# Triangular inverse in a gated DeltaNet kernel: masks applied to the products, refinement in 16-bit halves

## The chip, the cores and the metric

One core of a Trainium2 chip runs the kernel. The metric is device microseconds of one execution, the median of three runs. A second execution was taken with the hardware profiler; its rows are what the text below reads.

## The reference, cut to what matters

The program is one layer of a hybrid encoder on 2048 prompt frames and 64 frames of a running stream (2112 tokens, width 1024). One projection feeds a gated DeltaNet group (4 heads of 128) and a pooling group; one output projection, a residual and a SwiGLU block follow. The change lies in the DeltaNet group, in the inverse of a unit triangular matrix that each chunk of tokens needs:

```python
gamma = jnp.exp(jnp.where(lower_incl, G[..., :, None] - G[..., None, :], -jnp.inf))
kb = k * beta[..., None]
Lm = jnp.where(lower_strict, jnp.einsum('bhncd,bhnsd->bhncs', kb, k) * gamma, 0.0)
T = lax.linalg.triangular_solve(eye + Lm, jnp.broadcast_to(eye, Lm.shape),
                                left_side=True, lower=True)
u = jnp.einsum('bhncs,bhnsv->bhncv', T, v * beta[..., None])
w = jnp.einsum('bhncs,bhnsk->bhnck', T, kb * jnp.exp(G)[..., None])
```

The kernel works on chunks of 128 tokens, so it needs the inverse of I + Lm, 128 x 128, once for each head and chunk: 16 chunks x 4 heads for the prompt, and two for the 64 frames of the stream, where two heads share a 128 x 128 matrix.

## The kernel before

The tokens go through in four blocks of 512 (the first has the 64 stream frames beside it). For each block the kernel projects one output tile of the input projection after the other (matmuls into `pp`), convolves and gates the four heads, and runs the DeltaNet group. The output projection of the block before (`pz`) lies between. All of this is the first stage. The second is the SwiGLU block in three blocks of 704 tokens (`px`, `py`, `pz`, `d`, `dx` with operands `h`, `ws`, `wsd`), which is built as a fast matrix product with seven products for eight.

A dense product is made of three float32r matmuls on high and low parts, 512 columns each in most blocks. In this text "dense" means these.

A `Front` does the work of two chunks of one head that needs no state: it transposes k (`ptk`), spreads the decay over the partitions (`gb`), forms Gam = exp of the decay differences, the products of k with q and k (`gr`), and from them U, the strictly triangular matrix (tile `Gst` in the profile) for both chunks side by side (128 x 2 x 128). There are 32 such fronts for the prompt, and one for the stream (`_s`). Then it inverts:

- Level l = 0 to 6 (0 to 5 for the stream) joins diagonal blocks of size 2^l to blocks twice as large. POOL multiplies U with the level's 0/1 mask into 16-bit `Um`; PE multiplies it with the present inverse T (`py`); ACT casts this to 16 bits (`Yt`); PE multiplies with V, the transposed inverse, for T and for V (`pt`, four products of 128 columns); DVE subtracts the result from T and V (`TV`, 128 x 512).
- Refinement: the residual F = I - T - U T in float32 (`pf`, two products), then V + F V and V + F (V + F V) in float32 (`px`, two and two products). The result X is float32.

A `Head` then runs over the chunks in order, with the state S (`pk`, `po`).

The order of instructions is not that of the code. Every operation is recorded with a rank; the fronts' operations have the highest priority (`hot`). Class `Machine` then runs a list scheduler over all records of the program: it has a cost for each kind of operation (a 128-column float32 product, for one, is dearer than a 16-bit one), gives each engine the ready operation with the best rank, lets TensorE take dense products while others are not ready, and writes out one fixed order for each engine. All instructions come from that one place, so that the profile gives them all the same line, L278; tiles tell them apart. A tile's name in the profile is the name in the code without numbers and tags: `Yt_p` is `Yt` of a prompt front. Each of the three front slots (`NLEV`) has one PSUM bank for all of `py`, `pt`, `pf` and `px`.

Of the kernel before, what the change touches and what calls it, by code (L numbers as in the profile page):

```python
# [18 lines left out]
P = 128  # L19
# [5 lines left out]
C = 128  # L25
# [330 lines left out]
def hybrid_kernel(ctx, tc, a, o):  # L356
    nc = machine = Machine(tc.nc)
    act = nc.scalar.activation
    tt = nc.vector.tensor_tensor
    ts = nc.vector.tensor_scalar  # L360
    stt = nc.vector.scalar_tensor_tensor
# [76 lines left out]
    cp1, gp = pool("cp1", p1, True), pool("gp", p1, True)  # L438
# [396 lines left out]
    nc.vector.tensor_copy(selp, names["sel"].unsqueeze(2))  # L835
    lm_f = gp.tile([P, 2, 512], F32, tag="Yqk", name="lm_f", bufs=NY).rearrange("p i (l n) -> p (i l) n", n=P)
    nc.sync.dma_start(out=lm_f, in_=a["lmask"])
    lmask = cp1.tile([P, 7, P], F16, tag="lmask", name="lmask")
    nc.vector.tensor_copy(lmask, lm_f[:, :7])
    negm = cp1.tile([P, P], BF16, tag="negm", name="negm")  # L840
    nc.vector.tensor_copy(negm, lm_f[:, 7])

# [17 lines left out]
    def bc(t, nch, n):  # L860
        return t.unsqueeze(1).to_broadcast([t.shape[0], nch, n])
# [4 lines left out]
    class Front:  # L866
# [43 lines left out]
        def all(self):  # L910
            tag, chunk = self.tag, self.chunk
            two = lambda ps: ps[:, : 2 * C].rearrange("p (c n) -> p c n", n=C)
            gt = lambda shape, dt, t, bufs, n="": gp.tile(shape, dt, tag=t, name=f"{t.split('_')[0]}{n}_{tag}", bufs=bufs)
            slot = self.i % NLEV
            lev = lambda dt, t, n="", shape=[P, 2, C], bufs=1: gt(shape, dt, f"{t}_{slot}", bufs, n)
            yield self.before(NOUT, "used")

            kn = self.kn = gt([P, 3, 2], F32, "kn", NOUT + 1)
            ktl = self.ktl = gt([P, 2, P], F32, "ktl", NOUT)
            ptr = self.ps(f"ptk_{tag}")  # L920
            for c in range(2):
                transpose(ptr[:, c * P : (c + 1) * P], chunk(1, c), ident)
            for c in range(2):
                act(ktl[:, c, :], ptr[:, c * P : (c + 1) * P], AF.Square, accum_out=kn[:, 2, c : c + 1])
            for c in range(2):
                act(ktl[:, c, :], ptr[:, c * P : (c + 1) * P], AF.Copy, scale=self.e(2)[:, c : c + 1])
            act(kn[:, 2], kn[:, 2], AF.Ln, bias=epsc)
            act(kn[:, 0], kn[:, 2], AF.Exp, scale=0.5)
            act(kn[:, 1], kn[:, 2], AF.Exp, scale=-1.0)
            tt(kn[:, 1], kn[:, 1], self.e(1), ALU.mult)  # L930
            ts(kn[:, 2], kn[:, 1], -1.0, None, ALU.mult)
            yield self.before(NLEV, "levels")
            TV32 = lev(F32, "TV32", "", [P, 2, 2, C])
            gb = self.ps(f"gb_{tag}")
            self.rowmm(gb)
            EG = TV32[:, 0]
            act(EG, two(gb), AF.Exp)
            EL = self.EL = gt([P, NH if self.h is None else 2, 1], F32, "EL", NOUT)
            n = DEC if self.h is None else C
            nc.gpsimd.tensor_copy(EL, EG.rearrange("p c n -> p (c n)").rearrange("p (e n) -> p e n", n=n)[:, :, n - 1 : n])  # L940
            Qd = self.Qd = gt([P, 2, C], F32, "Qd", NOUT)
            tt(Qd, self.Yqk[:, 0, self.off : self.off + 2 * C].rearrange("p (c n) -> p c n", n=C), EG, ALU.mult)

            mm(gb[:, : 2 * C], idbf, bc(negm2 if self.h is None else negm, 2, C), start=False, stop=True,
               skip_group_check=True)
            Gam = self.QKG = gt([P, 2, C], F32, "Gam", NOUT)
            for c in range(2):
                act(Gam[:, c], gb[:, c * C : (c + 1) * C], AF.Exp, bias=self.fall()[:, c : c + 1])
            U = lev(F32, "Gst")
            nc.gpsimd.tensor_tensor(out=U, in0=Gam, in1=bc(ident, 2, C), op=ALU.subtract)  # L950
            yield LAT_G
            ps = self.ps(f"gr_{tag}")
            for c in range(2):
                ck = slice(self.off + c * C, self.off + (c + 1) * C)
                mm(ps[:, c * 2 * C : (c + 1) * 2 * C], chunk(1, c), self.Yqk[:, :, ck], start=True, stop=True)
            v = ps.rearrange("p (c t n) -> p c t n", t=2, n=C)
            for c in range(2):
                stt(U[:, c], v[:, c, 1, :], kn[:, 1, c : c + 1], U[:, c], ALU.mult, ALU.mult)
            tt(Gam, v[:, :, 0, :], Gam, ALU.mult)
            yield LAT_G  # L960

            TV = None
            nlev = n.bit_length() - 1
            for l in range(nlev):
                Um = lev(F16, "Um", l, bufs=2)
                nc.gpsimd.tensor_tensor(out=Um, in0=U, in1=bc(lmask[:, l], 2, C), op=ALU.mult)
                new = TV32 if l == nlev - 1 else lev(F16, f"TV{l % 2}", l, [P, 2, 2, C])
                py = self.ps(f"py{l}_{tag}")  # L970
                for c in range(2):
                    mm(py[:, c * C : (c + 1) * C], Um[:, c], id16 if l == 0 else TV[:, 0, c], start=True, stop=True)
                if l == 0:
                    idb = bc(id16, 2, C)
                    tt(new[:, 0], idb, two(py), ALU.subtract)
                    nc.gpsimd.tensor_tensor(out=new[:, 1], in0=idb, in1=Um, op=ALU.subtract)
                else:
                    Yt = lev(F16, "Yt", l)
                    nc.scalar.copy(Yt, two(py))
                    yield LAT_A  # L980
                    pt = self.ps(f"pt{l}_{tag}")
                    for c in range(2):
                        mm(pt[:, c * C : (c + 1) * C], TV[:, 1, c], Yt[:, c], start=True, stop=True)
                    for c in range(2):
                        mm(pt[:, (c + 2) * C : (c + 3) * C], Yt[:, c], TV[:, 1, c], start=True, stop=True)
                    tt(new, TV, pt.rearrange("p (t c n) -> p t c n", t=2, n=C), ALU.subtract)
                TV = new
                yield LAT_TV
            T, V = TV32[:, 0], TV32[:, 1]

            F = lev(F32, "TV0", "F")
            nc.gpsimd.tensor_tensor(out=F, in0=bc(ident, 2, C), in1=T, op=ALU.subtract)
            pf = self.ps(f"pf_{tag}")
            for c in range(2):
                mm(pf[:, c * C : (c + 1) * C], U[:, c], T[:, c], start=True, stop=True)
            tt(F, F, two(pf), ALU.subtract)
            yield LAT_F
            px = self.ps(f"px0_{tag}")
            for c in range(2):
                mm(px[:, c * C : (c + 1) * C], F[:, c], V[:, c], start=True, stop=True)  # L1000
            tt(T, V, two(px), ALU.add)
            yield LAT_D
            yield self.before(NX, "used")
            X = self.X = gt([P, 2, C], F32, "X", NX)
            px = self.ps(f"px1_{tag}")
            for c in range(2):
                mm(px[:, c * C : (c + 1) * C], F[:, c], T[:, c], start=True, stop=True)
            tt(X, V, two(px), ALU.add)
            self.levels = True

            ptr2 = self.ps(f"ptv_{tag}")
            vtk = self.vtk = gt([P, 2, P], F32, "vtk", NX)
            for c in range(2):
                transpose(ptr2[:, c * P : (c + 1) * P], chunk(2, c), ident)
            for c in range(2):
                act(vtk[:, c, :], ptr2[:, c * P : (c + 1) * P], AF.Copy, scale=kn[:, 0, c : c + 1])
            yield LAT_D
            self.done = True
# [401 lines left out]
    for k in (4, 5, 6, 7, 0, 1, 2, 3):  # L1420
        t = wpool.tile([P, 512], F32, tag="xc", name=f"od{k}", bufs=XBUFS["xc"])
# [271 lines left out]
def _layout(inp):  # L1693
# [51 lines left out]
    lm = np.zeros((P, 8, P), f32)  # L1745
    for l in range(7):
        s = 1 << l
        lm[:, l, :] = (i[:, None] // (2 * s) == i[None] // (2 * s)) & (i[:, None] // s < i[None] // s)
    lm[:, 7, :] = np.where(i[None] >= i[:, None], 0.0, -1e30)
    r["lmask"] = lm  # L1750
    z = np.zeros((P, 12), f32)
# [47 lines left out]
```

## Time and profile before

| | |
|---|---|
| median of three runs | 2381.3 us (2381.26 to 2382.45) |
| span of the profiled execution, first to last instruction | 2378.0 us |
| granted TensorE clock over the span | 0.998 |
| level and refinement work, first to last | 68 to 930 us |
| first product of the SwiGLU stage | 977.9 us |
| busy: TensorE, VectorE, ScalarE, GpSimd | 98%, 75%, 54%, 43% |

No total of the profiled execution other than its span is at hand; the difference of 3.3 us to the median is what the runs count before and after the first and last instruction. PE is TensorE, PEld its weight loads, DVE VectorE, ACT ScalarE, POOL GpSimd. A row of a group reads: operation, written tile, read tiles, shape and type, count, busy time in us, mean duration in ns, idle time of the engine just before these and what ended it. A row of the timeline has the start in us, the time that the merged instructions cover, and their count; a number in brackets is idle time before. A float32 product of 128 columns has two records, a 16-bit one has one. Matmuls overlap in the pipeline, so their cost is read from start to start.

### The profile page before, as it was taken

Reading aid. Unit: us, or ns where it says so; the run is one execution under the profiler, and the core shown is the slowest. Engines: PE = TensorE matmul, PEld = TensorE weight load, DVE = VectorE, ACT = ScalarE, POOL = GpSimd, SP = SyncE. Lnnn points to the kernel's source line nnn. Section 1 sums busy time; section 2 is a strip of 40 time slices with the busy share of each in tenths; the row PEclk is TensorE's granted clock in tenths of the full one; section 3 lists DMA queues with packets and bytes.
Section 4 is the critical chain, followed back from the end, with each engine's and each line's share of the span. In section 5 each row is a group of like instructions: output and inputs, shape, how many; then the busy total and the mean of one; then the engine's idle time right before and its main releaser. Section 6 shows DMA issues by size and latency. Waiting matters only on the chain. (4 is left out here: it accounts for less than half of the span.)

```text
span 2378.0 us, 41860 instructions
## 1 busy us (share of the span) xinstructions
PE 2331.7 (98%) x14679; PEld 2176.7 (92%) x14679; DVE 1775.5 (75%) x3096; ACT 1288.2 (54%) x2920; POOL 1011.0 (43%) x1160
## 2 busy tenths in 40 slices
PE   8999999999999999999999999999999999999998
PEld 8898898878787868999999999999999999999998
DVE  8998875775677786788676764878777778777666
ACT  6766745572647464574453555664444564545444
POOL 3756633553357552354232225554323563323122
PEclk9999999999999999999999999999999999999999
DMA  8744565545555565887654556766744586454653
GB/s 292 250 152 164 164 226 207 174 153 183 170 196 181 174 197 161 307 284 240 211 182 169 186 194 228 255 218 194 254 163 149 168 292 215 148 180 161 201 177 107
DMA packets 218883, 471.37 MB, mean 198 GB/s; under 512 B 27185, under 2 KB 85553, under 8 KB 218673
## 3 DMA queue, kind: packets, MB, share of 16 engines
q1 hardware_dynamic: 218672, 468.71, 58.9%
q8 instruction: 115, 1.88, 0.3%
q14 instruction: 96, 0.78, 0.1%
HBM read 354.81 MB, written 113.80 MB: 197 GB/s over the span
## 5 line engine op out<-in xcount | busy, mean ns | idle before, releaser
L278 PE MATMUL pp<-h,wsp 128*128 128x512 f32 (+1 forms) x2480 | 560.6, 366 | 10.3 <-DVE wsp L278 9.8
L278 PEld LDWEIGHTS pp<-h,wsp 128*128 128x128 f32 x2480 | 401.5, 190 | 57.0 <-ACT wsp L278 9.2
L278 POOL TENSOR_TENSOR Um_p<-Gst_p,lmask 128x256 f16<-128x256 f32 x224 | 181.3, 823 | 98.6 <-PE py_p L278 76.3
L278 ACT CAST ws<-wr 128x512 fp32r<-128x512 f32 x198 | 121.9, 618 | 175.5 <-PE dx L278 50.0
L278 DVE TENSOR_TENSOR ws<-wr,ws 128x512 fp32r<-128x512 f32 x198 | 168.1, 851 | 55.3 <-ACT ws L278 51.0
L278 PE MATMUL pz<-op,wsp 128*128 128x288 f32 (+1 forms) x768 | 170.0, 358 | 1.0 <-ACT op L278 0.5
L278 PE MATMUL d<-h,wsd 128*128 128x352 f32 x1056 | 170.0, 322 | 0.0
L278 PEld LDWEIGHTS d<-h,wsd 128*128 128x128 f32 x1056 | 168.7, 188 | 0.1
L278 DVE TENSOR_TENSOR TV_p<-TV_p,pt_p 128x512 f16<-128x512 f16 x192 | 129.3, 680 | 33.2 <-PE pt_p L278 31.4
L278 ACT ACTIVATE hr<-g 128x352 f32<-128x352 f32 x132 | 65.6, 497 | 158.9 <-DVE g L278 158.6
L278 POOL TENSOR_TENSOR wrS<-wr,wrS 128x512 f32<-128x512 f32 x44 | 64.9, 1476 | 196.5 <-DMA wrS<-in_wu_dram 65.8
L278 PE MATMUL px<-hA,ws 128*128 128x352 f32 x792 | 145.0, 322 | 0.6 <-DVE ws L278 0.6
L278 PE MATMUL px<-hBT,wsS 128*128 128x352 f32 x792 | 139.8, 324 | 5.5 <-ACT g L278 5.0
L278 PE MATMUL py<-hB,wsS 128*128 128x352 f32 x792 | 143.6, 322 | 0.0
L278 PE MATMUL pz<-hB,ws 128*128 128x352 f32 x792 | 142.0, 322 | 0.0
L278 PE MATMUL py<-hA,wsS 128*128 128x352 f32 x792 | 140.0, 322 | 0.0
L278 PE MATMUL px<-hBT,ws 128*128 128x352 f32 x792 | 138.4, 323 | 1.5 <-DVE u L278 1.4
L278 PE MATMUL px<-hA,wsS 128*128 128x352 f32 x792 | 137.9, 322 | 1.4 <-ACT g L278 1.3
L278 PEld LDWEIGHTS px<-hBT,wsS 128*128 128x128 f32 x792 | 128.0, 188 | 10.7 <-ACT g L278 10.7
L278 POOL TENSOR_TENSOR q<-hr,hr 128x352 f32<-128x352 f32 x40 | 44.0, 1099 | 216.2 <-DVE hr L278 214.7
L278 PEld LDWEIGHTS pz<-op,wsp 128*128 128x128 f32 x768 | 120.6, 190 | 12.3 <-DVE wsp L278 0.8
L278 PEld LDWEIGHTS px<-hBT,ws 128*128 128x128 f32 x792 | 128.4, 188 | 3.4 <-DVE u L278 3.2
(672 smaller groups left out, 5858.0 us busy)
## 6 DMA issues: line engine op xcount, KB each, us to landing
wsS<-gS SPq DMA_DIRECT2D x176, 512.0 KB, 4.5
wsp<-wnd SPq DMA_DIRECT2D x126, 512.0 KB, 3.3
gS<-wsS SPq DMA_DIRECT2D x88, 512.0 KB, 4.3
wr<-in_wg_dram SPq DMA_DIRECT2D x132, 256.0 KB, 3.0
wnd<-wsp SPq DMA_DIRECT2D x42, 512.0 KB, 5.0
xd<-x2d SPq DMA_DIRECT2D x96, 176.0 KB, 3.4
wr<-in_wu_dram SPq DMA_DIRECT2D x66, 256.0 KB, 3.4
wrd<-in_wd_dram SPq DMA_DIRECT2D x56, 256.0 KB, 3.0
```

What stands on the lines that cost most here:

```text
L278: getattr(getattr(self.nc, op.eng), name)(*args, **kw)
```

## The change

The diagonal is put into the matrix: U becomes 2048 (I + Lm)^T, with POOL's addition of a scaled identity (`idw`), and ACT casts it once to 16 bits (`Wh`); POOL forms the low half `Wl` = U - `Wh`. Every level multiplies the whole `Wh` with T, and DVE applies the level's mask when it takes the product out of PSUM. The masks are now I minus the 0/1 block mask, divided by 2048, so that the masked product is the factor with which T and V are multiplied; `pt` then gives the new T and V themselves, and ACT casts them out of PSUM (128 x 512). T and V stay in 16 bits at the last level too. An eighth mask, the transpose of level 0's, is made once by one product.

The refinement: `pf` = `Wh` T + `Wl` T in four 16-bit products; F = I - pf/2048 on DVE; F scaled by 256 is split into a high half (ACT) and a low half (DVE); `px` = F V in four 16-bit products; ACT casts it (`YtF`), and two further products with the high half accumulate F F V onto it; DVE adds V. The result X is float32 as before.

```diff
@@ setup
-    lmask = cp1.tile([P, 7, P], F16, tag="lmask", name="lmask")
-    nc.vector.tensor_copy(lmask, lm_f[:, :7])
+    lmask = cp1.tile([P, 8, P], F16, tag="lmask", name="lmask")
+    nc.vector.tensor_copy(lmask[:, :7], lm_f[:, :7])
...
+    idw = cp1.tile([P, P], F16, tag="idw", name="idw")
+    ts(idw, ident, WSCALE, None, ALU.mult)
+    pm = bank(0, "pm")
+    mm(pm[:, :P], lmask[:, 0], id16, start=True, stop=True)
+    nc.scalar.copy(lmask[:, 7], pm[:, :P])
@@ Front.all
-            tt(kn[:, 1], kn[:, 1], self.e(1), ALU.mult)
-            ts(kn[:, 2], kn[:, 1], -1.0, None, ALU.mult)
+            stt(kn[:, 1], kn[:, 1], WSCALE, self.e(1), ALU.mult, ALU.mult)
+            ts(kn[:, 2], kn[:, 1], -1.0 / WSCALE, None, ALU.mult)
...
+            nc.gpsimd.tensor_tensor(out=U, in0=U, in1=bc(idw, 2, C), op=ALU.add)
+            Wh = lev(F16, "Wh")
+            nc.scalar.copy(Wh, U)
...
             for l in range(nlev):
-                Um = lev(F16, "Um", l, bufs=2)
-                nc.gpsimd.tensor_tensor(out=Um, in0=U, in1=bc(lmask[:, l], 2, C), op=ALU.mult)
-                new = TV32 if l == nlev - 1 else lev(F16, f"TV{l % 2}", l, [P, 2, 2, C])
+                new = lev(F16, f"TV{l % 2}", l, [P, 2, 2, C])
                 py = self.ps(f"py{l}_{tag}")
                 for c in range(2):
-                    mm(py[:, c * C : (c + 1) * C], Um[:, c], id16 if l == 0 else TV[:, 0, c], start=True, stop=True)
+                    mm(py[:, c * C : (c + 1) * C], Wh[:, c], id16 if l == 0 else TV[:, 0, c], start=True, stop=True)
+                Z = new[:, 0] if l == 0 else lev(F16, "Yt", l)
+                tt(Z, two(py), bc(lmask[:, l], 2, C), ALU.mult)
                 if l == 0:
-                    idb = bc(id16, 2, C)
-                    tt(new[:, 0], idb, two(py), ALU.subtract)
-                    nc.gpsimd.tensor_tensor(out=new[:, 1], in0=idb, in1=Um, op=ALU.subtract)
+                    nc.gpsimd.tensor_tensor(out=new[:, 1], in0=Wh, in1=bc(lmask[:, 7], 2, C), op=ALU.mult)
                 else:
-                    Yt = lev(F16, "Yt", l)
-                    nc.scalar.copy(Yt, two(py))
...
-                    tt(new, TV, pt.rearrange("p (t c n) -> p t c n", t=2, n=C), ALU.subtract)
+                    nc.scalar.copy(new, pt.rearrange("p (t c n) -> p t c n", t=2, n=C))
+                if l == 1:
+                    Wl = lev(F16, "Wl")
+                    nc.gpsimd.tensor_tensor(out=Wl, in0=U, in1=Wh, op=ALU.subtract)
...
-            F = lev(F32, "TV0", "F")
-            nc.gpsimd.tensor_tensor(out=F, in0=bc(ident, 2, C), in1=T, op=ALU.subtract)
             pf = self.ps(f"pf_{tag}")
             for c in range(2):
-                mm(pf[:, c * C : (c + 1) * C], U[:, c], T[:, c], start=True, stop=True)
-            tt(F, F, two(pf), ALU.subtract)
+                for w in (Wh, Wl):
+                    mm(pf[:, c * C : (c + 1) * C], w[:, c], T[:, c], start=w is Wh, stop=w is Wl)
+            F = lev(F32, "TV32", "F")
+            stt(F, two(pf), -1.0 / WSCALE, bc(ident, 2, C), ALU.mult, ALU.add)
+            FF = lev(F16, f"TV{nlev % 2}", "F", [P, 2, 2, C])
+            act(FF[:, 0], F, AF.Copy, scale=FSCALE)
+            stt(FF[:, 1], F, FSCALE, FF[:, 0], ALU.mult, ALU.subtract)
...
-                mm(px[:, c * C : (c + 1) * C], F[:, c], V[:, c], start=True, stop=True)
-            tt(T, V, two(px), ALU.add)
...
-                mm(px[:, c * C : (c + 1) * C], F[:, c], T[:, c], start=True, stop=True)
-            tt(X, V, two(px), ALU.add)
+                for i in range(2):
+                    mm(px[:, c * C : (c + 1) * C], FF[:, i, c], V[:, c], start=c == i == 0, stop=i == 1,
+                       skip_group_check=c > 0)
+            FV = lev(F16, "Yt", "F")
+            act(FV, two(px), AF.Copy, scale=1.0 / FSCALE)
+            yield LAT_D
+            for c in range(2):
+                mm(px[:, c * C : (c + 1) * C], FF[:, 0, c], FV[:, c], start=False, stop=True, skip_group_check=True)
+            stt(X, two(px), 1.0 / FSCALE, V, ALU.mult, ALU.add)
@@ host tables
+WSCALE, FSCALE = 2048.0, 256.0
...
-        lm[:, l, :] = (i[:, None] // (2 * s) == i[None] // (2 * s)) & (i[:, None] // s < i[None] // s)
+        lm[:, l, :] = (i[:, None] == i[None]) * 1.0 - ((i[:, None] // (2 * s) == i[None] // (2 * s)) & (i[:, None] // s > i[None] // s))
+        lm[:, l, :] /= WSCALE
```

The scheduler's costs and rules stay as they are; since the operations differ, it writes another order. First TensorE's order where the residual of one front is formed (third block, second head, first two chunks), before. `TV_p_1_0` is that front's T and V, `pz` the dense product between:

```order
L278 MATMUL pz_4_0_1786<-op_1_1229,wsp_64_1701 128x512 x3
L278 MATMUL pk_p_0_1_1834<-Sp,Yqk_0_1518 128x128
L278 MATMUL pf_p_1_0_1837<-TV_p_1_0_1709,Gst_p_1_0_1714 128x128 x2
L278 LDWEIGHTS TV_p_1_1_1825
L278 MATMUL pt_p_1_1_1844<-Yt_p_1_1_1841,TV_p_1_1_1825 128x128
```

The same place after the change:

```order
L278 MATMUL pt_p_1_1_1770<-TV_p_1_1_1747,Yt_p_1_1_1768 128x128
L278 LDWEIGHTS Wh_p_1_0_1673
L278 MATMUL pf_p_1_0_1777<-TV_p_1_0_1763,Wh_p_1_0_1673 128x128
L278 LDWEIGHTS Wl_p_1_0_1704
L278 MATMUL pf_p_1_0_1777<-TV_p_1_0_1763,Wl_p_1_0_1704 128x128
```

Two float32 products with U became 16-bit ones with `Wh` and `Wl` (four in all, two for each chunk), right behind the 16-bit `pt` of the neighbouring front.

Second, ScalarE's order at the end of the same front, before:

```order
L278 CAST Yt_p_1_1_1827<-py_p_1_1_1826 128x256
L278 ACTIVATE vn_p_0_1_1820<-pk_p_0_1_1816,kn_p_0_1_1609 128x128
L278 CAST Yt_p_1_0_1823<-py_p_1_0_1822 128x256
L278 CAST Yt_p_1_1_1841<-py_p_1_1_1840 128x256
L278 ACTIVATE vn_p_0_1_1842<-pk_p_0_1_1834,kn_p_0_1_1609 128x128
```

and after:

```order
L278 CAST TV_p_1_0_1763<-pt_p_1_0_1769 128x512
L278 CAST TV_p_1_1_1766<-pt_p_1_1_1770 128x512
L278 ACTIVATE TV1F_p_1_0_1779<-TV32F_p_1_0_1778 128x256
L278 ACTIVATE vn_p_0_1_1783<-pk_p_0_1_1771,kn_p_0_1_1558 128x128
L278 ACTIVATE YtF_p_1_0_1787<-px_p_1_0_1786 128x256
```

ScalarE now takes `pt` (512 columns) instead of `py` (256 columns), and has two casts of the refinement beside the head's `vn`.

Third, GpSimd's order at the start of a front of the first block (fourth head, first two chunks), before:

```order
L278 TENSOR_TENSOR Gst_p_3_0_684<-Gam_p_3_0_683,consts 128x256
L278 TENSOR_TENSOR Um_p_3_0_714<-Gst_p_3_0_684,lmask 128x256
L278 TENSOR_TENSOR Um_p_3_0_729<-Gst_p_3_0_684,lmask 128x256
L278 TENSOR_TENSOR TV_p_3_0_715<-id_144,Um_p_3_0_714 128x256
L278 TENSOR_TENSOR Um_p_3_0_749<-Gst_p_3_0_684,lmask 128x256
L278 TENSOR_TENSOR Um_p_3_0_767<-Gst_p_3_0_684,lmask 128x256
```

and after:

```order
L278 TENSOR_TENSOR Gst_p_3_0_669<-Gam_p_3_0_668,consts 128x256
L278 TENSOR_TENSOR osq_p_1__603<-osq_p_1__603,Yvz_1_200 128x512
L278 TENSOR_TENSOR Gst_p_3_0_669<-Gst_p_3_0_669,idw 128x256
L278 TENSOR_TENSOR TV_p_3_0_704<-Wh_p_3_0_696,lmask 128x256
L278 TENSOR_TENSOR Wl_p_3_0_727<-Gst_p_3_0_669,Wh_p_3_0_696 128x256
```

One product with a mask for each level became three operations per front, all near its start.

More of the change, by code (lines that the diff above doesn't have):

```diff
@@ L929, in all @@
             act(kn[:, 1], kn[:, 2], AF.Exp, scale=-1.0)
-            tt(kn[:, 1], kn[:, 1], self.e(1), ALU.mult)
-            ts(kn[:, 2], kn[:, 1], -1.0, None, ALU.mult)
+            stt(kn[:, 1], kn[:, 1], WSCALE, self.e(1), ALU.mult, ALU.mult)
+            ts(kn[:, 2], kn[:, 1], -1.0 / WSCALE, None, ALU.mult)
             yield self.before(NLEV, "levels")
-            TV32 = lev(F32, "TV32", "", [P, 2, 2, C])
+            EG = lev(F32, "TV32", "")
             gb = self.ps(f"gb_{tag}")
             self.rowmm(gb)
-            EG = TV32[:, 0]
             act(EG, two(gb), AF.Exp)
@@ L958, in all @@
                 stt(U[:, c], v[:, c, 1, :], kn[:, 1, c : c + 1], U[:, c], ALU.mult, ALU.mult)
+            nc.gpsimd.tensor_tensor(out=U, in0=U, in1=bc(idw, 2, C), op=ALU.add)
+            Wh = lev(F16, "Wh")
+            nc.scalar.copy(Wh, U)
             tt(Gam, v[:, :, 0, :], Gam, ALU.mult)
             yield LAT_G
-            TV = None
             nlev = n.bit_length() - 1
             for l in range(nlev):
-                Um = lev(F16, "Um", l, bufs=2)
-                nc.gpsimd.tensor_tensor(out=Um, in0=U, in1=bc(lmask[:, l], 2, C), op=ALU.mult)
-                new = TV32 if l == nlev - 1 else lev(F16, f"TV{l % 2}", l, [P, 2, 2, C])
+                new = lev(F16, f"TV{l % 2}", l, [P, 2, 2, C])
                 py = self.ps(f"py{l}_{tag}")
                 for c in range(2):
-                    mm(py[:, c * C : (c + 1) * C], Um[:, c], id16 if l == 0 else TV[:, 0, c], start=True, stop=True)
+                    mm(py[:, c * C : (c + 1) * C], Wh[:, c], id16 if l == 0 else TV[:, 0, c], start=True, stop=True)
+                Z = new[:, 0] if l == 0 else lev(F16, "Yt", l)
+                tt(Z, two(py), bc(lmask[:, l], 2, C), ALU.mult)
                 if l == 0:
-                    idb = bc(id16, 2, C)
-                    tt(new[:, 0], idb, two(py), ALU.subtract)
-                    nc.gpsimd.tensor_tensor(out=new[:, 1], in0=idb, in1=Um, op=ALU.subtract)
-                else:
-                    Yt = lev(F16, "Yt", l)
-                    nc.scalar.copy(Yt, two(py))
+                    nc.gpsimd.tensor_tensor(out=new[:, 1], in0=Wh, in1=bc(lmask[:, 7], 2, C), op=ALU.mult)
+                else:
                     yield LAT_A
@@ L982, in all @@
                     for c in range(2):
-                        mm(pt[:, c * C : (c + 1) * C], TV[:, 1, c], Yt[:, c], start=True, stop=True)
+                        mm(pt[:, c * C : (c + 1) * C], TV[:, 1, c], Z[:, c], start=True, stop=True)
                     for c in range(2):
-                        mm(pt[:, (c + 2) * C : (c + 3) * C], Yt[:, c], TV[:, 1, c], start=True, stop=True)
-                    tt(new, TV, pt.rearrange("p (t c n) -> p t c n", t=2, n=C), ALU.subtract)
+                        mm(pt[:, (c + 2) * C : (c + 3) * C], Z[:, c], TV[:, 1, c], start=True, stop=True)
@@ L987, in all @@
+                    nc.scalar.copy(new, pt.rearrange("p (t c n) -> p t c n", t=2, n=C))
+                if l == 1:
+                    Wl = lev(F16, "Wl")
+                    nc.gpsimd.tensor_tensor(out=Wl, in0=U, in1=Wh, op=ALU.subtract)
                 TV = new
                 yield LAT_TV
-            T, V = TV32[:, 0], TV32[:, 1]
-            F = lev(F32, "TV0", "F")
-            nc.gpsimd.tensor_tensor(out=F, in0=bc(ident, 2, C), in1=T, op=ALU.subtract)
+            T, V = TV[:, 0], TV[:, 1]
@@ L993, in all @@
             pf = self.ps(f"pf_{tag}")
             for c in range(2):
-                mm(pf[:, c * C : (c + 1) * C], U[:, c], T[:, c], start=True, stop=True)
-            tt(F, F, two(pf), ALU.subtract)
-            yield LAT_F
-            px = self.ps(f"px0_{tag}")
-            for c in range(2):
-                mm(px[:, c * C : (c + 1) * C], F[:, c], V[:, c], start=True, stop=True)
-            tt(T, V, two(px), ALU.add)
-            yield LAT_D
+                for w in (Wh, Wl):
+                    mm(pf[:, c * C : (c + 1) * C], w[:, c], T[:, c], start=w is Wh, stop=w is Wl)
@@ L1003, in all @@
+            F = lev(F32, "TV32", "F")
[3 more added lines that the diff above has]
+            stt(FF[:, 1], F, FSCALE, FF[:, 0], ALU.mult, ALU.subtract)
+            yield LAT_F
             yield self.before(NX, "used")
             X = self.X = gt([P, 2, C], F32, "X", NX)
-            px = self.ps(f"px1_{tag}")
+            px = self.ps(f"px_{tag}")
```

## The prediction

> **What bounds the kernel now.** I read the page first, then busy time by stage, then TensorE's waits, then its instructions one by one.
>
> ```profile
> PE 2331.7 (98%) x14679; PEld 2176.7 (92%) x14679; DVE 1775.5 (75%) x3096; ACT 1288.2 (54%) x2920; POOL 1011.0 (43%) x1160
> ```
>
> TensorE (PE) is busy for 98% of the span; no other engine comes near over the whole. An average hides stages, so here is the same by stage: length, then busy time of PE, weight loads, DVE, ACT and POOL, then granted clock and DMA share.
>
> ```profile
> 70.00:200.00 130.00, 127.62 (x1037) 118.46 (x1036) 125.36 (x259) 94.34 (x255) 85.11 (x119) 1.00 0.59 199
> 200.00:300.00 100.00, 98.66 (x660) 82.45 (x658) 90.08 (x165) 64.56 (x153) 66.05 (x80) 1.00 0.51 169
> 300.00:800.00 500.00, 498.68 (x3150) 419.10 (x3148) 337.82 (x614) 269.31 (x695) 233.19 (x328) 1.00 0.54 183
> 800.00:900.00 100.00, 93.29 (x509) 73.77 (x508) 86.00 (x139) 58.91 (x146) 60.68 (x71) 0.97 0.67 204
> 900.00:978.00 78.00, 78.00 (x432) 66.07 (x431) 55.91 (x100) 39.11 (x84) 15.91 (x15) 1.00 0.66 207
> 978.00:2378.00 1400.00, 1376.30 (x8497) 1359.93 (x8495) 1023.08 (x1687) 713.13 (x1470) 522.42 (x496) 1.00 0.60 201
> ```
>
> Everything that the change touches ends by 978 us; from there the SwiGLU stage runs, whose rows on PE stand in the same order in both programs. Up to 978 PE is the bound too: the five rows hold 11.7 us without PE work (908 less 896.3). From 70 to 300 us DVE runs close behind, at 215 of 230 us. What PE waited for from 10 to 970 us (total, times, longest; the five largest):
>
> ```profile
> PE pt_p L278 <- ACT Yt_p L278: 3.7, 4, 2.0
> PE py_p L278 <- DVE TV_p L278: 2.2, 2, 1.9
> PE gb_p L278 <- ACT ktl_p L278: 1.9, 4, 0.6
> PE pf_p L278 <- DVE TV_p L278: 1.3, 2, 0.7
> PE pp L278 <- DVE wsp L278: 0.6, 1, 0.6
> ```
>
> 9.7 us, and little behind them. So hundreds of handovers between the level products and ACT or DVE cost PE some 7 us in all: the list scheduler puts dense matmuls (pp, pz) into the gaps. A microsecond of PE work taken out before 978 us is then a microsecond of time, and the sum below is one of PE work.
>
> **Removed and added on PE.** Now the price of one product. First how many float32 products the refinement has, then PE's starts around one front.
>
> ```profile
> L278 PE MATMUL px_p<-TV_p,TV0F_p 128*128 128x128 f32 x256 | 40.2, 278 | 0.0
> L278 PE MATMUL pf_p<-TV_p,Gst_p 128*128 128x128 f32 x128 | 21.1, 284 | 1.3 <-DVE TV_p L278 1.3
> ...
> 661.72 0.61 PE L278 MATMUL px_p<-TV_p,TV0F_p 128*128 128x128 f32 x4
> 662.16 0.28 PE L278 MATMUL pt_p<-Yt_p,TV_p 128*128 128x128 f16 x2
> 662.27 0.28 PE L278 MATMUL pt_p<-TV_p,Yt_p 128*128 128x128 f16 x2
> 662.38 0.66 PE L278 MATMUL px_p<-TV_p,TV0F_p 128*128 128x128 f32 x4
> ...
> 820.69 0.38 PE L278 MATMUL pk_p<-vn_p,ktl_p 128*128 128x128 f32 x2
> 820.91 0.39 PE L278 MATMUL po_p__2584<-Gam_p,vn_p 128*128 128x128 f32 x2
> 821.05 2.78 PE L278 MATMUL pp<-h,wsp 128*128 128x512 f32 x11
> 823.67 0.38 PE L278 MATMUL pk_p<-Sp,Yqk 128*128 128x128 f32 x2
> ...
> 849.14 0.29 PE L278 MATMUL py_p<-TV_p,Um_p 128*128 128x128 f16 x2
> 849.24 1.86 PE L278 MATMUL pp<-h,wsp 128*128 128x512 f32 x7
> 850.94 0.23 PE L278 MATMUL pt_p<-Yt_p,TV_p 128*128 128x128 f16 x1
> ```
>
> 384 records over 32 fronts are twelve for six products: a float32 product is two records. The busy times (278 ns) overlap, so I take start to start. From 661.72 to 662.16 two float32 products take 0.44 us; from 820.69 to 820.91 one takes 0.22. Two 16-bit products take 0.11 (662.16 to 662.27): 0.055 each, with new weights for each. The 33 fronts (32 and the sample's) lose 6 x 33 = 198 float32 products, 198 x 0.22 = 43.6 us, and gain 10 x 33 + 1 = 331 16-bit ones, 331 x 0.055 = 18.2. The level products keep their number and size. Net -25.4 us.
>
> Changing the kind of product costs too. Eleven dense matmuls take 2.62 us up to a float32 product and seven take 1.70 up to a 16-bit one, so one is 0.23 and entering either kind costs 0.09. Going back is cheaper: after a float32 product dense work starts 0.14 later instead of 0.22 (-0.08), after 16-bit ones 0.10 instead of 0.11 (-0.01). Counted in the two orders, PE leaves dense work for 16-bit products 273 times instead of 180 and for float32 ones 179 instead of 264 (+8 x 0.09 = +0.7), returns from 16-bit ones 302 times instead of 267 (-0.4) and from float32 ones 149 instead of 176 (27 x 0.08 = +2.2). Together +2.5.
>
> **Moved between the other engines.** The rows with the prices:
>
> ```profile
> L278 DVE TENSOR_TENSOR TV_p<-TV_p,pt_p 128x512 f16<-128x512 f16 x160 | 108.0, 680 | 27.6 <-PE pt_p L278 26.1 <-POOL Um_p L278 1.2
> L278 DVE TENSOR_TENSOR TV_p<-id,py_p 128x256 f16<-128x256 f16 x32 | 13.1, 410 | 0.5 <-PE py_p L278 0.5
> L278 DVE TENSOR_TENSOR TV_p<-TV_p,px_p 128x256 f32<-128x256 f32 x32 | 13.3, 416 | 8.0 <-PE px_p L278 7.4
> L278 DVE SCALAR_TENSOR_TENSOR h<-x,nw,h 128x288 fp32r<-128x288 f32 x16 | 7.1, 511 | 4.7 <-ACT h L278 4.7
> L278 ACT CAST Yt_p<-py_p 128x256 f16<-128x256 f32 x192 | 70.4, 373 | 110.4 <-PE py_p L278 110.0
> L278 ACT COPY ext<-pp 128x512 f32<-128x512 f32 x36 | 20.9, 579 | 19.0 <-PE pp L278 18.8
> L278 ACT CAST wsp<-wrp 128x256 fp32r<-128x256 f32 x4 | 1.4, 403 | 0.4 <-DMA wrp<-in_win_dram 0.4
> L278 ACT ACTIVATE E<-E,onec 128x512 f32<-128x512 f32 x64 | 46.8, 732 | 1.3
> L278 POOL TENSOR_TENSOR Um_p<-Gst_p,lmask 128x256 f16<-128x256 f32 x224 | 181.3, 823 | 98.6 <-PE py_p L278 76.3 <-DVE Gst_p L278 21.1 <-POOL Um_p L278 0.3
> ```
>
> - DVE, per front: six 128x512 updates (6 x 0.68) go and six masked products of half the width come (6 x 0.41). The three narrow adds of the refinement (0.416) become three scalar_tensor_tensor of 256 columns; no row has that shape, the 288-column one (0.511) is the ceiling, a 256-column add at 0.41 the floor, and I take 0.47. -1.5 us a front.
> - ACT: six casts (0.373) become six of twice the width out of PSUM (0.579), and three of 256 columns are new (0.37 to 0.403). +2.4 us a front, 80 in all, over a stage in which ACT works 526 of 908 us.
> - POOL: seven mask products and F go, the addition of idw and Wl come; the start of V stays. Six fewer at 0.823: -5 us a front.
> - A level's chain stays as long: cast 0.373 and update 0.68 before, mask 0.41 and cast 0.579 now. The front's start gets an ACT cast longer (U, idw on POOL, Wh on ACT, where U, Um stood), its end a cast and a DVE step longer between pf and px (+0.4 + 0.47). Both lie on the front's own chain, and dense matmuls cover that as they now cover each level's cast and update; without cover PE would pay up to 33 x 1.3 = 43 us. Behind a cast that waits for py or pt stand silu's E (up to 0.73) and the copies that free PSUM for pp.
> - The set-up's one product, its copy to the eighth mask and idw lie in the first 45 us beside dense work: 0, at most their own microsecond. No DMA is added or moved past another, and the mask table keeps its size.
>
> **The sum.** -25.4 + 2.5 = -22.9. Of the waits, 7.2 us belong to handovers that now change engines; I take 1 us off, since POOL's mask products drop out and DVE is relieved where it ran at 215 of 230 us. The span of 2378.0 becomes 2354.1; the median of the runs, 2381.3, lies 3.3 above that span, and I keep the difference: 2357.
>
> **A page against a row.** How fast 16-bit products with new weights each can follow one another decides most of the added term; this is the weight load's row (count, least, median and longest ns):
>
> ```profile
> L278 PEld LDWEIGHTS <-Yt_p x384: 95/98/147, 73.1 to 922.9; 128*128 128x128 f16 x192
> ```
>
> The loads are longer than the 0.055 between starts, yet the starts are 0.055 apart: they overlap. The Trainium skill ("TensorE: Matmul & The Clock Gate", Back-to-back issue gap) states about 81 ns a product for a stream of load and matmul pairs at 128 columns. By it the added term would be an estimated 331 x 0.081 = 26.8 and the time 2366; the trace's 0.055 disagrees.
>
> **Rivals.**
> 1. *The load sets the pace after all*, in these pairs of high and low halves: 331 x 0.098 = 32.4, net -11.2 + 2.5 - 1, 2372. Against it stands every pair of pt above. The Trainium skill's figure above leans this way. 0.04.
> 2. *ACT answers late* (the other side). Place: the cast of pt to the new T and V, 197 times, on which the next py waits; an E of 0.73 may stand ahead of it. From 70 to 200 us ACT goes from 94 of 130 us to about 109 of 125. Price: if PE stands for an E at a quarter of them, 50 x 0.73 = 36 us, and the time is 2393; it decides from 24 us, 0.12 a handover. A wait also costs afterwards:
>
> ```profile
> 803.61 0.39 PE L278 MATMUL po_p__2584<-Gam_p,vn_p 128*128 128x128 f32 x2
> 805.99 0.27 PE L278 MATMUL pt_p<-Yt_p,TV_p 128*128 128x128 f16 x2 [2.00 <-ACT Yt_p L278]
> ...
> 806.18 2.25 PE L278 MATMUL pp<-h,wsp 128*128 128x512 f32 x5
> 808.23 0.63 PE L278 MATMUL pk_p<-Sp,Yqk 128*128 128x128 f32 x2
> ```
>
>    After 2 us of idleness five dense matmuls took 2.05 us up to the next float32 product instead of 5 x 0.23 + 0.09 = 1.24. Against it: the same handover runs through ACT now, 192 times, and cost 3.7 us in four waits, while ACT idled 110 us for py. 0.20, in which 0.07 ends still faster, 0.06 within the bound, 0.07 slower.
> 3. *More comes than the products*: lighter DVE and POOL end nearly all waits in the stage, 10 us and a microsecond of slow clock: 2346. For it, 215 of 230 us on DVE; against it, ACT's load. 0.14.
> 4. *The saving lies off the path from 70 to 300 us*, since DVE is the bound there. Some nine fronts run in that stretch, 9 x 0.7 = 6 us lost: 2363. DVE loses 1.5 us where PE loses 0.7, so it should not; I count it inside the forecast's own range.
>
> **How the numbers follow.** 0.62 for the forecast, 2357, whose own range is 2351 to 2364 (rival 4 above; a float32 product at 0.225 and three more waits gone below). The range of 8 in 10 reaches from rival 3 to rival 1: 2345 to 2372. 0.2% is 4.8 us, about what a measurement of this kernel can tell from no change. Faster by more: 0.62 + 0.14 + 0.04 + 0.07 = 0.87; within: 0.06; slower: 0.07.
>
> **What would show it.** PE's records pf_p and px_p are f16, in pairs 0.11 apart; the SwiGLU stage starts near 954 us instead of 978 and lasts 1400 again; PE's waits before it stay near 12 us; ACT's busy time rises by some 80 us, DVE's falls by some 50 and POOL's by some 160. Wrong would be a row of PE waiting for ACT's TV_p or YtF_p with tens of microseconds, 16-bit pairs 0.16 apart or more, or a later stage that grows.

## The result, and the profile after

The changed kernel takes 2344.9 us (median of 4 runs, 2343.8 to 2345.7) against 2381.3 beside it: ratio 0.985 (0.984 to 0.986). That is 36.4 us less where 24 were forecast: on the lower edge of the range of 8 in 10 (2345 to 2372) and below the forecast's own range (2351 to 2364). Its profiled execution has a span of 2342.9 us, 35.1 less than before, and a granted clock of 0.999.

The page's first line (busy time and share of the span, engine by engine):

```profile
PE 2304.3 (98%) x14614; PEld 2139.1 (91%) x14614; DVE 1688.4 (72%) x3097; ACT 1357.9 (58%) x3020; POOL 840.9 (36%) x963
```

ACT gained 70 us of work; DVE lost 87 and POOL 170. By stage (length, then busy PE, weight loads, DVE, ACT, POOL, clock, DMA share, GB/s):

```profile
70.00:200.00 130.00, 128.50 (x1092) 118.94 (x1092) 120.72 (x278) 110.12 (x283) 56.54 (x90) 1.00 0.64 204
200.00:300.00 100.00, 98.18 (x667) 81.10 (x665) 83.44 (x172) 78.00 (x188) 34.57 (x50) 1.00 0.53 173
300.00:800.00 500.00, 498.55 (x3146) 405.69 (x3146) 301.52 (x619) 313.90 (x742) 159.22 (x232) 1.00 0.58 187
800.00:900.00 100.00, 98.64 (x608) 77.85 (x607) 75.89 (x153) 68.08 (x166) 33.08 (x38) 1.00 0.68 203
900.00:947.00 47.00, 47.00 (x209) 38.84 (x208) 37.01 (x60) 26.23 (x54) 7.27 (x5) 1.00 0.87 277
947.00:2342.90 1395.90, 1374.86 (x8497) 1360.41 (x8495) 1013.46 (x1683) 713.09 (x1469) 522.90 (x496) 1.00 0.61 202
```

PE is the bound as before. From 800 to 900 us it works 98.6 of 100 us at full clock, where it had 93.3 at 0.97. The SwiGLU stage starts at 947.0 (least, median, longest ns; first and last start; its row is the one below) and lasts 1395.9 us, 4.2 less than before:

```profile
L278 PE MATMUL px<-hA,ws x792: 317/322/429, 947.0 to 2288.4; 128*128 128x352 f32 x198
```

What PE waited for before that (total, times, longest):

```profile
PE pt_p L278 <- DVE Yt_p L278: 1.8, 4, 0.6
PE pp L278 <- DVE h L278: 1.1, 2, 0.7
PE py_p L278 <- ACT TV_p L278: 1.1, 4, 0.5
PE pp L278 <- DVE wsp L278: 1.1, 2, 0.6
PE px_p L278 <- ACT TV1F_p L278: 0.7, 2, 0.5
```

All rows of this view from 43 to 940 us add up to 7.0 us, against 12.1 in the kernel before. This total is used for every experiment below.

The new products on PE's timeline:

```profile
665.35 0.22 PE L278 MATMUL pf_p<-TV_p,Wh_p 128*128 128x128 f16 x1
665.40 0.22 PE L278 MATMUL pf_p<-TV_p,Wl_p 128*128 128x128 f16 x1
665.46 0.22 PE L278 MATMUL pf_p<-TV_p,Wh_p 128*128 128x128 f16 x1
665.51 0.22 PE L278 MATMUL pf_p<-TV_p,Wl_p 128*128 128x128 f16 x1
665.57 0.28 PE L278 MATMUL py_p<-TV_p,Wh_p 128*128 128x128 f16 x2
...
673.69 0.28 PE L278 MATMUL px_p<-YtF_p,TV1F_p 128*128 128x128 f16 x2
673.81 0.44 PE L278 MATMUL pk_p<-rhs_p,X_p 128*128 128x128 f32 x2
```

Four products of pf take 0.22 us, two of px 0.12: 0.055 to 0.06 each. And the moved work, as groups (mean ns of one, then the engine's idle time before and what ended it):

```profile
L278 ACT CAST TV_p<-pt_p 128x512 f16<-128x512 f32 x192 | 111.2, 590 | 62.2 <-PE pt_p L278 61.6
L278 DVE TENSOR_TENSOR Yt_p<-py_p,lmask 128x256 f16<-128x256 f32 x192 | 78.9, 419 | 46.5 <-PE py_p L278 46.2
L278 DVE SCALAR_TENSOR_TENSOR TV1F_p<-TV32F_p,TV1F_p 128x256 f16<-128x256 f32 x32 | 16.8, 528 | 6.0 <-ACT TV1F_p L278 6.0
```

The prices of the level's cast and mask are those of the forecast (0.579 and 0.41 us). The step that makes F's low half took 0.528, where the forecast had 0.47 and 0.511 as a ceiling; over 33 fronts that is 2 us of DVE. Before these casts and masks ACT and DVE stand idle until PE delivers, for 62 and 46 us; PE stood 1.1 and 1.8 us for them.

**Where the 35 us of the span went.** For every kind of record on PE I took the usual start-to-start time, given the kinds before and behind it (over the traces of before and after), and multiplied by how often each stands in the fixed order. That is an estimate of the stage's PE work; the rest up to the first SwiGLU product is standing time, with what a wait leaves behind in slower matmuls. PE work fell from 953.0 to 932.5 us (-20.5; the forecast had -22.9), standing time from 15.7 to 5.2 (-10.5; the forecast had -1), and the SwiGLU stage lost 4.2 (forecast: nothing). So the products came nearly as forecast, and some 15 us more came from elsewhere. The experiments ask from where.

### The profile page after: what moved, and what is told of

It is laid out like the page before. It is cut to its first block, busy times and chain, and to the rows that moved or that the text cites. A ratio compares the mean times of both kernels' runs of the same rounds, so it can differ in the third digit from the quotient of the medians.

```text
span 2342.9 us, 41453 instructions
## 1 busy us (share of the span) xinstructions
PE 2304.3 (98%) x14614; PEld 2139.1 (91%) x14614; DVE 1688.4 (72%) x3097; ACT 1357.9 (58%) x3020; POOL 840.9 (36%) x963
## 5 line engine op out<-in xcount | busy, mean ns | idle before, releaser
L278 ACT CAST TV_p<-pt_p 128x512 f16<-128x512 f32 x192 | 111.2, 590 | 62.2 <-PE pt_p L278 61.6
L278 PEld LDWEIGHTS px<-hA,ws 128*128 128x128 f32 x792 | 129.9, 188 | 1.2 <-DVE ws L278 1.1
L278 PEld LDWEIGHTS px<-hA,wsS 128*128 128x128 f32 x792 | 128.7, 188 | 2.0 <-ACT g L278 2.0
L278 PEld LDWEIGHTS py<-hB,wsS 128*128 128x128 f32 x792 | 129.9, 188 | 0.0
```

What stands on the lines that cost most here:

```text
L278: getattr(getattr(self.nc, op.eng), name)(*args, **kw)
```

## The experiments

Theory A: the surplus comes from lighter DVE and POOL, which no longer keep PE waiting. Theory B: it is the luck of a new order. The texts set off below were written before each run. Unless said otherwise times are medians, with the ratio to runs of the kernel before on the same chip (their median was 2380.4 to 2380.7).

**Each half alone.** The new levels with the float32 refinement:

```diff
-                new = lev(F16, f"TV{l % 2}", l, [P, 2, 2, C])
+                new = TV32 if l == nlev - 1 else lev(F16, f"TV{l % 2}", l, [P, 2, 2, C])
...
-                for w in (Wh, Wl):
-                    mm(pf[...], w[:, c], T[:, c], start=w is Wh, stop=w is Wl)
+                mm(pf[...], U[:, c], T[:, c], start=True, stop=True)
...
```

> The new levels (masks on the product, cast of T and V on ACT) with the float32 refinement of before. The float32 products all stay, so the products' 22.9 us are not in it; from the counted changes of kind, -1.4 us. Theory A (what came beyond 23 us came from the levels: lighter DVE and POOL, fewer waits of PE near the end of the first stage): 2381 - 1 - 13 = 2367. Theory B (the levels do nothing, it all lies in the refinement): 2380. Theory C (the surplus is how one fixed order happens to fall at the end of the first stage, and belongs to neither part): anywhere from 2368 to 2388, and the two halves do not add up to the whole.

2373.3 us, 0.997 (0.996 to 0.998): 7 us gained with PE work unchanged (953.0); PE's waits are 9.1 us instead of 12.1. Only the range of theory C holds this. And the old levels with the 16-bit refinement, as excerpts of the difference from the changed kernel:

```diff
+                Um = lev(F16, "Um", l, bufs=2)
+                nc.gpsimd.tensor_tensor(out=Um, in0=U, in1=bc(lmask[:, l], 2, C), op=ALU.mult)
...
-                tt(Z, two(py), bc(lmask[:, l], 2, C), ALU.mult)
+                nc.scalar.copy(Yt, two(py))
...
-                nc.scalar.copy(new, pt...)
+                tt(new, TV, pt..., ALU.subtract)
...
```

> The levels of before (POOL masks, DVE subtracts) with the 16-bit refinement; U carries the factor 2048 without the identity, POOL forms I - T, ACT one more cast. Products -25.4 us, changes of kind by the counts of its order +5.7: 2362 if nothing else moves. Theory A: 2362. Theory B: 2345 to 2350. Theory C: 2350 to 2370, with the gain or loss beyond 20 us in the last block before the SwiGLU stage and in that stage's first 100 us.

2371.9 us, 0.996 (0.995 to 0.998). PE has 19 us less work here (933.8), but only 8.6 us came out, less than any of the three theories had. Its waits, the largest rows:

```profile
PE pt_p L278 <- ACT Yt_p L278: 3.0, 6, 0.7
PE gb_p L278 <- ACT ktl_p L278: 2.2, 5, 0.6
PE py_p L278 <- DVE TV_p L278: 1.7, 5, 0.9
PE pz L278 <- DVE op L278: 1.5, 2, 1.0
```

Nothing stands out; many small rows grew together, to 17.8 us. The halves gave 16 us, the whole 36; that they don't add up is what theory C had said.

**Order.** Every edit makes the scheduler write a new order of the whole stage. How much an order is worth, I asked with the same instructions and one planning constant moved by 3 or 4%:

```diff
-LAT_SILU = 7.08
+LAT_SILU = 7.3
```

> The changed kernel with one planning constant moved by 3% (LAT_SILU 7.08 to 7.3), same instructions in another order. Theory A (the work decides, not the order): 2345 within 3 us. Theory B (the order is worth as much as the surplus of 12 us): 2350 to 2360.

> The kernel before with the same constant moved (LAT_SILU 7.08 to 7.3). Theory A: 2381 within 3 us. Theory B: anywhere from 2368 to 2392; below 2375 would say that the order of before was an unlucky one.

```diff
-LAT_G = 4.53
+LAT_G = 4.7
```

> The changed kernel with another planning constant moved by 4% (LAT_G 4.53 to 4.7). Theory A: 2345 within 3 us. Theory B: 2350 to 2360.

The changed kernel took 2352.2 (0.988, 0.986 to 0.989) and 2355.2 us (0.989, 0.987 to 0.990), the kernel before 2380.4 (1.000, 0.999 to 1.001). The three orders of the changed kernel have the same instructions and the same PE work (932.5, 931.8, 932.3 us). What differs are PE's waits: 7.0, 11.7 and 12.5 us, and the standing time with all that follows from them: 5.2, 10.7 and 15.3. A single wait reaches 2.5 us in the one and 1.4 in the other, against 0.7 in the order that was built; here is that of the LAT_G order on PE's timeline (the bracket is the idle time):

```profile
850.24 0.27 PE L278 MATMUL pt_p<-Yt_p,TV_p 128*128 128x128 f16 x2 [1.40 <-DVE Yt_p L278]
```

So 7 to 10 us of the 36 belong to the one order that was built, and theory B holds for these. The kernel before, with the one constant moved, stayed within 1 us, as its theory A had it, so the spread is not the same for every kernel. Both constants were moved up and neither down: whether the built order is a lucky one, or these constants suit the changed kernel, is not shown.

The halves in the other order as well:

```diff
-LAT_SILU = 7.08
+LAT_SILU = 7.3
```

> The new levels with the float32 refinement (2373.3 us), in another order (LAT_SILU 7.08 to 7.3). If the levels' own gain (7 us against before) is more than the order's spread of 10 us among the changed kernel's three orders: 2370 to 2377. If it was luck: up to 2383.

> The old levels with the 16-bit refinement (2371.9 us), in another order (LAT_SILU 7.08 to 7.3). PE has 19 to 20 us less work in it than before the change. If what it lost of that (11 us of new waits) was an unlucky order: 2358 to 2366. If DVE and POOL, as loaded as before, do not let PE run faster: 2368 to 2376.

2370.5 us (0.996, 0.995 to 0.998) and 2366.7 (0.995, 0.994 to 0.997). So levels alone bring 7 and 10 us, the refinement alone 9 and 14, the whole 36, 28 and 25. In the means over the orders that is 9, 11 and 30. What comes only when both halves are there is poorly known from these totals: 20 us with the constants as built (36 less 7 and 9), some 5 with LAT_SILU at 7.3 (28 less 10 and 14).

PE work of the refinement kernel is some 20 us lower in both its orders, its standing time 28.6 and 27.6 us against 15.7 and 16.6 in the two orders of before: some 12 of the 20 us come back as standing time. Its second time, 2366.7, lies between what was expected of an unlucky order and of engines that don't answer sooner, so the time alone doesn't decide. The first block of tokens does. This is its length, from the first product `pc` of that block to the first of the next:

| | in each order, us |
|---|---|
| before | 202.0, 203.0 |
| new levels alone | 201.4, 199.3 |
| 16-bit refinement alone | 202.3, 203.1 |
| both | 194.7, 195.2, 195.7 |

Here the orders of one kernel differ by 2 us at most, and the pattern is the same in all. The refinement alone takes some 5 us of PE work out of this block (by the estimate), and none of it comes out as time. On top of the new levels the same refinement brings 4 to 7 us. In this block DVE is busy 191 of 202 us and POOL 123, before and with the refinement alone; with both halves they are busy 179 and 76 of 195. The block in the kernel before, with the refinement alone and with both halves (length, then busy PE, weight loads, DVE, ACT, POOL, clock, DMA share, GB/s):

```profile
43.00:245.00 202.00, 197.67 (x1546) 180.68 (x1545) 191.05 (x403) 136.33 (x360) 123.39 (x172) 1.00 0.57 193
43.10:245.30 202.20, 194.50 (x1518) 171.19 (x1517) 191.16 (x389) 144.07 (x380) 123.26 (x179) 1.00 0.58 195
43.00:238.00 195.00, 191.03 (x1534) 173.70 (x1533) 178.68 (x410) 154.34 (x390) 76.44 (x123) 1.00 0.61 200
```

So in this block the surplus is not luck: while DVE and POOL are loaded as before, PE can't use what it saves. The refinement's longer chain and its casts on ACT stand in the kernel with both halves too, so they aren't the reason. Which of the two engines it is, these runs don't tell.

**POOL.** The changed kernel with 230 dead mask products, one at each level, read by nobody:

```diff
+                Um = lev(F16, "Um", l, bufs=2)
+                nc.gpsimd.tensor_tensor(out=Um, in0=U, in1=bc(lmask[:, l], 2, C), op=ALU.mult)
```

> The changed kernel with the mask products of before still issued on POOL (one for each level and front, 230 in all, 0.68 to 1.2 us each), into a tile that nothing reads. PE, ACT and DVE have the same operations as in the changed kernel. If POOL's relief (its own queue, or what it takes from DVE's second SBUF input) gave the surplus: 2353 to 2358. If POOL does not matter: 2345, within 2 us, apart from what another order does.

2362.3 us, 0.992 (0.991 to 0.994): 17 us lost against the order that was built and 7 to 10 against the two others, in an order that the scheduler made for this load. That is more than either expectation had. As that again mixes load and order, the next run keeps the order: the dead products cost nothing in the scheduler's reckoning, and the orders of PE, DVE, ACT and SP are the changed kernel's row for row. Each reads the level's own mask result, so that it falls beside its level.

```diff
+                Um = lev(F16, "Um", l, bufs=2)
+                machine.dead = True
+                nc.gpsimd.tensor_tensor(out=Um, in0=U, in1=Z, op=ALU.mult)
+                machine.dead = False
```

> The changed kernel with 230 dead products added on POOL (128x256, two inputs in SBUF, about 0.8 us each, one beside every level, written to a tile that nobody reads), kept out of the scheduler's reckoning: the order of PE, DVE, ACT and SP is the changed kernel's, row for row. Theory A (the gain beyond the products came from a lighter POOL, which no longer stands in DVE's way): the order explains nothing, POOL's load alone costs most of what it cost with a newly made order (17.4 us), so 2355 to 2364; DVE's instructions with two inputs in SBUF get 8 to 10% longer again. Theory B (the surplus is the luck of a new order): 2345 to 2349. In between: both.

2376.2 us, 0.998 (0.997 to 0.999): 31 us lost, more than expected. PE's waits are 24.9 us instead of 7.0. The first block alone takes 211.1 us instead of 194.7, more than half of the loss; POOL is busy 128 us there, where it was 76. The groups (POOL's added work, DVE's convolution taps), then what DVE and PE waited for:

```profile
L285 POOL TENSOR_TENSOR Um_p<-Gst_p,Yt_p 128x256 f16<-128x256 f32 x192 | 158.8, 833 | 123.4 <-DVE Yt_p L285 117.2 <-DVE kn_p L285 2.9 <-DMA xc<-in_xT_dram 2.5
L285 DVE SCALAR_TENSOR_TENSOR Yqk<-ext,consts,Yqk 128x512 f32<-128x512 f32 x96 | 87.5, 912 | 8.3 <-ACT Yqk L285 6.9
```

```profile
DVE pd L285 <- POOL pw L285: 13.1, 8, 3.3
...
PE pt_p L285 <- DVE Yt_p L285: 4.9, 10, 1.1
PE ptk_p L285 <- DVE Yqk L285: 3.3, 4, 1.7
PE pt_s L285 <- DVE Yt_s L285: 2.9, 1, 2.9
PE py_p L285 <- ACT TV_p L285: 2.8, 6, 1.1
```

The same rows of the changed kernel, taps and DVE's wait, and the taps of the kernel before:

```profile
L278 DVE SCALAR_TENSOR_TENSOR Yqk<-ext,consts,Yqk 128x512 f32<-128x512 f32 x96 | 80.3, 837 | 8.5 <-ACT Yqk L278 7.0
```

```profile
DVE pd L278 <- POOL pw L278: 7.1, 6, 2.1
```

```profile
L278 DVE SCALAR_TENSOR_TENSOR Yqk<-ext,consts,Yqk 128x512 f32<-128x512 f32 x96 | 87.5, 913 | 10.6 <-ACT Yqk L278 9.7
```

Two things happen at once. The same tap, with two inputs in SBUF, takes 913 ns on average before, 837 after, and 912 with POOL's load put back, while DVE's work on 128x256 out of PSUM stays at 410 to 420 ns in all three. And POOL's later work comes late: the pooling step `pd` stands 13.1 us on DVE for POOL's `pw` instead of 7.1, and PE waits longer for DVE's `Yt` and for the taps' `Yqk`; that these are late because of what stands before them on DVE is argued, not shown. To tell these apart, two dead copies with one 16-bit input take the place of each product:

```diff
-                nc.gpsimd.tensor_tensor(out=Um, in0=U, in1=Z, op=ALU.mult)
+                nc.gpsimd.tensor_copy(Um, Z)
+                nc.gpsimd.tensor_copy(Um, Z)
```

> As the run with 230 dead products on POOL in the changed kernel's own order (2376.2 us), but each dead product is replaced by two dead copies (128x256, one 16-bit input, about 0.4 us each by the 0.34 to 0.35 us of POOL's small copies and up): about the same time on POOL's queue, without a second input in SBUF. If POOL's queue is what hurts (later work of POOL starts late): 2365 to 2376, as there. If it is the second input that stands in DVE's way: 2345 to 2355, and DVE's taps back near 837 ns.

2373.2 us, 0.997 (0.996 to 0.998). The groups, and DVE's longest wait:

```profile
L285 POOL COPY Um_p<-Yt_p 128x256 f16<-128x256 f16 x384 | 206.9, 543 | 106.9 <-DVE Yt_p L285 94.6
L285 DVE SCALAR_TENSOR_TENSOR Yqk<-ext,consts,Yqk 128x512 f32<-128x512 f32 x96 | 81.9, 854 | 8.4 <-ACT Yqk L285 6.8
```

```profile
DVE Yt_p L285 <- POOL Um_p L285: 15.3, 20, 1.9
```

The taps are nearly as short as without the load (854 ns), though the low-half step of F is as long as beside the products (581 and 582 ns, 528 without load), and the time is nearly as bad. So a loss of this size does not need a second input on POOL; a POOL that is late is enough. How the two share it in the run with products stays open: the copies took 543 ns instead of the 400 that I had reckoned with, POOL's added load is thus 242 us instead of 187, and DVE now waits 15.3 us for the copies themselves to let go of the mask result (1.7 us in the run with products). And both runs keep an order that didn't reckon with the load; where it did, the cost was the 17 us above, or 7 to 10.

**DVE.** Is ACT the right place for the cast of pt?

```diff
-                    nc.scalar.copy(new, pt.rearrange("p (t c n) -> p t c n", t=2, n=C))
+                    nc.vector.tensor_copy(new, pt.rearrange("p (t c n) -> p t c n", t=2, n=C))
```

> The changed kernel with the cast of pt to T and V on DVE instead of ACT: DVE gets 197 casts of 512 columns (some 0.6 us each, 119 us in all), ACT loses as much. If ACT answering late holds PE up in the changed kernel, this is faster, 2335 to 2342. Theory A (DVE's relief is part of the gain): the nine fronts from 70 to 300 us add some 32 us to a DVE that is busy 204 of 230 us there, so PE waits there: 2350 to 2365, with the loss before 300 us. If neither engine matters: 2345.

2367.7 us, 0.994 (0.992 to 0.996): 23 us lost against the order that was built, 13 to 15 against the two others. The group of the cast, and the two largest of PE's waits:

```profile
L278 DVE CAST TV_p<-pt_p 128x512 f16<-128x512 f32 x192 | 130.0, 684 | 19.9 <-PE pt_p L278 18.6
```

```profile
PE py_p L278 <- DVE TV_p L278: 3.4, 6, 1.5
PE gb_p L278 <- ACT ktl_p L278: 3.1, 5, 1.3
```

DVE is idle before these casts for only 19.9 us (ACT's cast has 62.2 above): it gets to them later. PE's waits are 17.3 us instead of 7.0, of which the cast's own row is 3.4. The loss is not all before 300 us, as expected: the first block, where DVE is busy 197 of 205 us, loses 10 us, and the last block before the SwiGLU stage another 9.

**The price of a product.** Four more products of `Wl` and T in each half of pf, outside the scheduler's reckoning:

```diff
-                for w in (Wh, Wl):
-                    mm(pf[...], w[:, c], T[:, c], start=w is Wh, stop=w is Wl)
+                mm(pf[...], Wh[:, c], T[:, c], start=True, stop=False)
+                machine.dead = True
+                for _ in range(4):
+                    nc.tensor.matmul(pf[...], Wl[:, c], T[:, c], start=False, stop=False)
+                machine.dead = False
+                mm(pf[...], Wl[:, c], T[:, c], start=False, stop=True)
```

> The changed kernel with the product of Wl and T in pf done five times instead of once (264 more 16-bit products of 128 columns, each with its own weight load, directly behind the others), kept out of the scheduler's reckoning, so that everything else stands in the changed kernel's order. It measures the price of one 16-bit product in its place. At the forecast's 0.055 us each: 2344.9 + 14.5 = 2359.4; at 0.081 (the Trainium skill's figure for a stream of such pairs): 2366.3; at the weight load's 0.098: 2370.8. If handovers behind pf were on the path too, more.

2355.4 us, 0.990 (0.988 to 0.991): 10.5 us for 264 products, 0.040 each.

```profile
672.48 0.44 PE L285 MATMUL pf_p<-TV_p,Wl_p 128*128 128x128 f16 x5
672.75 0.22 PE L285 MATMUL pf_p<-TV_p,Wh_p 128*128 128x128 f16 x1
672.81 0.44 PE L285 MATMUL pf_p<-TV_p,Wl_p 128*128 128x128 f16 x5
```

Five products, each with its own weight load, take 0.27 us, 0.054 each, so PE has 14.3 us more to do. PE's waits fell from 7.0 to 4.8 us, which accounts for 2.2 of the 3.8 us that are missing; the other 1.6 are within the 1 to 2 us by which runs of one kernel differ.

## Why the prediction was right, and where its size was off

- **PE is the bound, and the products' sum.** Held. PE work fell by 20.5 us in the order that was built and by 21.2 and 20.7 in the two others, where the sum had 22.9; which of its terms had the 2 us too many was not followed up. The 0.055 for a 16-bit product with new weights was measured again as 0.054. The rival in which the weight load sets the pace (2372) is out. In this kernel's bursts, up to 26 products in a row in the run with the added ones, the pairs stay 0.054 to 0.056 apart. The 81 ns of the Trainium skill's "TensorE: Matmul & The Clock Gate", Back-to-back issue gap, do not hold here: by them the 264 products would have cost an estimated 21.4 us; they cost 10.5.
- **"A microsecond of PE work taken out is a microsecond of time."** This held for the whole change, not for its refinement half: there 19 us of PE work gave 9 to 14 us of time. The step was read from 9.7 us of waits in an order made for the old PE load. In the first block the refinement alone gave no time at all: there PE's saving needs the relief of DVE and POOL that the levels bring, and the forecast had put that relief at 1 us.
- **Waits, -1 us.** This is the term that was mis-sized: in the order that was built the standing time fell by 10.5 us and the SwiGLU stage by 4.2. In the two other orders it was 5.0 and 0.7, and 0.4 and 1.8. PE's waits there are 11.7 and 12.5 us, which is the "near 12" of the forecast, and their times, 2352 and 2355, lie in the forecast's own range. So the forecast describes the change; that the measured time lies at the edge of its range is due to the order that was built, some 7 to 10 us better than its two neighbours. The prediction had no term for the spread of orders, in either direction.
- **More than the products (the rival at 2346).** Its time is what came, and its mechanism is half shown: with POOL's load put back the kernel is slower than in any of the three orders, by 7 to 17 us, but two of these orders, with the same light POOL, keep all of their waits.
- **ACT answers late (2393).** Out. ACT does 110 of 130 us from 70 to 200, as forecast, and PE waited 1.1 us for its `TV`. ACT at 85% cost PE next to nothing here; DVE with the same cast cost 13 to 23 us.
- **The saving lies off the path from 70 to 300 us (2363).** Out for the whole change: the first block is 7 us shorter in all three orders, more than its share of the products (a quarter of 22.9, 5.7). But its mechanism is real, as the refinement alone shows, whose saving in that block is lost. The prediction's argument against it, that DVE loses more work there than PE, is what the runs bear out.
- **Busy times.** ACT +70 (80 forecast), POOL -170 (160), DVE -87 instead of -50. Of these 37 us, 14 are no work that went: the taps on `Yqk` lost 7.2 us by being shorter, those on `Yvz` as much (920 to 774 ns). Another 10 lie in the SwiGLU stage (1023.1 to 1013.5); the rest was not followed up.
- **The SwiGLU stage "lasts 1400 again".** It lasted 1395.9, 1399.4 and 1398.3 in the three orders, 1400 in both of before. The three runs that keep the built order have 1395.7 to 1397.0, whatever their load, which points to the order; what in it does this is not shown.

## What to carry to other kernels

Here a saving on an engine that is busy 98% of the time came out in full only where the engines that feed it were relieved as well: in the most loaded block one half of the change gave 0 us, the other 1 to 4, both together 7 to 8. So look by stage for what a change takes from the other engines. Where a scheduler writes the order anew for each edit, the spread of orders belongs in the range of every forecast (here 10 us of 2350 among three orders of the changed kernel, 1 us between two of the kernel before). A comparison of two edits needs two or three orders of each, a stretch in which the orders agree, or an experiment that keeps the order. A helper engine can set the time through its queue though its average is low: POOL was busy 36% of the span, and 187 us of dead work added to it, with all other orders kept, cost 31, half of it in a block where it was then busy 61%.

## What the hardware showed that I had not expected

- DVE's instructions with two inputs in SBUF got longer as POOL worked: 837 ns became 912 for the same tap with 187 us of two-input products on POOL, and 854 with 242 us of one-input 16-bit copies. Another one, F's low-half step, went from 528 ns to 582 and 581, alike in both. DVE's work on 128x256 out of PSUM did not change (410 to 420 ns). In the kernels with a mask product on POOL at every level the tap took 912 to 936 ns, whatever the order, and in those without 814 to 862.
- POOL's copy of 256 columns in 16 bits took 543 ns; a product of two inputs of that width 833. Two copies are dearer than one product.
